# Delta-rule blocks: k-k and k-q products by halves with the heads alternating and fillers pinned between their turns, and three small moves of loads and copies

## The chip, the cores and the metric

The kernel runs on one core of a Trainium2 chip. The metric is the device time of one execution in microseconds (us). Before the change the median of three runs is 1339.09 us (1338.87 to 1339.35). The engines of the core run their own instruction streams in order: TensorE (PE) multiplies, VectorE (DVE), ScalarE (ACT) and GpSimd (POOL) do the rest, and SyncE (SP) and ScalarE issue the DMA transfers.

## The reference, cut to what matters

A block of a transformer with two mixers side by side: eight heads of dilated attention and eight heads of a gated delta rule, then a gated feed-forward part. The change lies in the delta rule and in the projections that run beside it.

```python
def reference(x, c, w_ada, ..., w_gate, w_up, w_down, final_norm_g):
    mod = c_act @ w_ada[l] + b_ada[l]
    h = _rmsnorm(x, norm_attn_g[l]) * (1.0 + sc1) + sh1
    proj = h @ w_in[l]
    q_a, k_a, v_a, q_d, k_d, v_d, z_d, b_d, a_d = jnp.split(proj, ...)
    y_attn = _dilated_attention(q_a, k_a, v_a, rel_bias)
    y_delta = _gated_deltanet(q_d, k_d, v_d, z_d, b_d, a_d, ...)
    x = x + g1 * (jnp.concatenate([y_attn, y_delta], axis=-1) @ w_out[l])
    h = _rmsnorm(x, norm_ffn_g[l]) * (1.0 + sc2) + sh2
    x = x + g2 * ((jax.nn.silu(h @ w_gate[l]) * (h @ w_up[l])) @ w_down[l])
    return _rmsnorm(x, final_norm_g)

def _gated_deltanet(q, k, v, z, ...):
    qkv = jax.nn.silu(_causal_conv(jnp.concatenate([q, k, v], axis=-1), conv_w))
    ...
    o = _chunk_gated_delta_rule(q, k, v, g, beta)
    return _rmsnorm(o, norm_g) * jax.nn.silu(z)

def _chunk_gated_delta_rule(q, k, v, g, beta):
    decay = jnp.where(causal, jnp.exp(gcum[..., :, None] - gcum[..., None, :]), 0.0)
    a_mat = jnp.where(strict, jnp.einsum('nbhcd,nbhed->nbhce', k_beta, kc) * decay, 0.0)
    sol = lax.linalg.triangular_solve(a_mat + eye, rhs, lower=True, ...)
    qk = jnp.where(causal, jnp.einsum('nbhcd,nbhed->nbhce', qc, kc) * decay, 0.0)
    ...
    _, o = lax.scan(step, state0, (qc, kc, u, w, gcum, qk))
```

There are 1024 tokens of 1024 features. A delta head has 64 features. The kernel works on chunks of 128 tokens where the reference has 64; the result is the same function.

## The kernel before, in words

**Groups.** The eight delta heads are worked on in two groups (g = 0 and 1) of four heads. A tile of k or q holds two heads, one on partitions 0 to 63 and the other on 64 to 127 (`kd[hp]`, `qd[hp]`), and eight chunks of 128 tokens along its rows. `delta(g)` runs: the convolutions and the transposes for the norms (`conv`, `delta_turn`), then `delta_prep`, `delta_v`, `delta_inverse` and `delta_scan`.

**The k-k and k-q products** (`delta_prep`, line 806). For each pair of heads q (two pairs in a group), for k-q ("q") and then k-k ("k"), for each half hf of the eight chunks, a turn of eight products of 64 x 128 by 64 x 128 is issued, four for each head e, into one PSUM bank for each head. Half 0 takes the two banks "s", half 1 the two banks "t". VectorE multiplies each full bank by the decay of that head (line 812). The decay is made in place in `lts` by 32 exponentials on ScalarE (line 776), head by head, eight chunks each. The finished k-k tiles go to DRAM (line 819) and come back as rows (`nt`, line 859). A program of 31 steps on VectorE (lines 905 and 909) inverts blocks of 32, its result goes to DRAM and comes back (`tn`, line 914), and four "heads" of small products (`lv`, `lw`, `lx`, lines 937 to 975) join the blocks on TensorE.

**Fillers.** Beside that run projections that don't depend on it: `others()` is a generator that issues matmuls of 512 or 256 columns (`gemm`, line 591, and `proj_t`, line 617) and yields after 0.64 or 0.32 us of them, in the order k and q of group 1, z of group 0, v of group 1, then v of the attention, z of group 1, k and q of the attention and so on. `turn(name)` first draws `FILL[name]` us out of this generator and then lets its instructions stand behind the last matmul drawn (`issue_after`). `hold(what, us)` at the start of the joining of the inverse draws until a projection is done and then `LEVELS` us more; the first product of the inverse stands behind that. `mixed()` also runs bursts of the modulation's matmuls after each 7.6 us of filler, unless `quiet` is set. What the delta part doesn't draw is drawn evenly by the attention (`attend`, constants `FRONT` and `BACK`).

**Order.** A scheduler takes the program's instructions by priority (the order of writing, `urgent()` puts them ahead) and puts each on its engine's stream when its operands are to be had in its own reckoning; the order on each engine is then fixed. Only `issue_after` pins an instruction behind another.

**The small places.** `z_evac` (line 638) copies a finished z block out of its PSUM bank through a Silu on ScalarE. `delta_early` starts the convolutions of group 1 (`cv0` to `cv3`) while group 0 inverts. `spill` (lines 1146 to 1151) copies projections of group 1 to DRAM. `out_delta` (lines 1475 to 1489) runs the delta half of the output projection during the attention: for each of eight row blocks d it splits a weight slab, and for each half it loads a block of x into `xo` (line 1482), multiplies, adds (line 1486) and stores. `xo`, `y_load`'s tiles and the first attention outputs share five buffers.

Of the kernel before, what the change touches and what calls it, by code (L numbers as in the profile page):

```python
# [10 lines left out]
F32 = mybir.dt.float32  # L11
# [20 lines left out]
LEVELS = ("z0", 4), ("z1", 24)  # L32
# [17 lines left out]
    "kk1_0_0_q": 6.4,  # L50
    "trq1_0False": 4.48,
    "trk1_0False": 1.92,
    "kk0_2_0_k": 1.28,
# [4 lines left out]
    "kk1_3_0_k": 0.64,  # L58
    "y0_0": 0.64,
    "trv3_0": 12.8,  # L60
    "kk1_0_0_k": 0.64,
# [5 lines left out]
    "kk0_0_0_k": 0.64,  # L67
}
for step in "abcd":
    for h in range(4):  # L70
        FILL.setdefault(f"l{step}0_{h}", 0.64)


def build(tc, I, out):
# [476 lines left out]
    def conv(ci, xp, dst):  # L551
        nc.scalar.activation(dst, xp, AF.Copy, scale=cw[:, ci, 3:4])
# [10 lines left out]
    used = [0.0]  # L563

# [18 lines left out]
    def gemm(ps, slabs, mh, ml, cs):  # L583
# [3 lines left out]
        for (wh, wl), k0 in slabs:  # L587
            for k4 in range(4):
                w0 = slice(k4 * P, (k4 + 1) * P)
                for a, b in ((wh, mh), (wh, ml), (wl, mh)):  # L590
                    last[0] = nc.tensor.matmul(ps, a[:, w0], b[k0 + k4][:, cs], start=(i == 0), stop=(i == n - 1))  # L591
                    i += 1
# [10 lines left out]
    def proj_t(src, n, name, evac, slabs=()):  # L603
# [5 lines left out]
        for tb in range(TB):  # L609
# [3 lines left out]
            for k in range(KT):  # L613
                wh, wl = slabs[k // 2]
                w0 = slice((k % 2) * n, (k % 2) * n + n)
                for a, b in ((hh, wh), (hl, wh), (hh, wl)):
                    last[0] = nc.tensor.matmul(ps[:, :n], a[k][:, ts_], b[:, w0], start=(i == 0), stop=(i == 23))  # L617
# [15 lines left out]

    def z_evac(g):
        def f(tb, ps):
            zt = pv.tile([P, 256], F32, name=f"zt{g}_{tb}", tag="ev", bufs=4)
            with urgent():
                taken[0] = nc.scalar.activation(zt, ps[:, 0:256], AF.Silu)  # L638
# [120 lines left out]
    def delta_prep(g, st, norms, kt, lts):  # L759
# [14 lines left out]
        for h in range(4):  # L774
            for n in range(8):
                nc.scalar.activation(lts[h][:, n], lts[h][:, n], AF.Exp, bias=lr[:, n, h : h + 1])
# [15 lines left out]
        qks = []  # L792
        for q in range(2):
# [3 lines left out]
            for dsts, mov, wh in ((two, qd[hp], "q"), (lts[2 * q : 2 * q + 2], kd[hp], "k")):  # L797
                for hf in range(2):

                    ps = [(sbank, tbank)[hf](f"kk{g}_{2 * q + e}_{hf}_{wh}") for e in range(2)]  # L800
                    with turn(f"kk{g}_{2 * q}_{hf}_{wh}"):
                        for j in range(4):
                            n = 4 * hf + j
                            for e in range(2):
                                rows = slice(64 * e, 64 * e + 64)
                                nc.tensor.matmul(
                                    ps[e][:, j * P : (j + 1) * P], kd[hp][rows, n * P : (n + 1) * P],
                                    mov[rows, n * P : (n + 1) * P], start=True, stop=True,
                                )
# [17 lines left out]

        for q in range(2):
# [310 lines left out]
    def spill(name, dst, scale=None):  # L1139
        def f(hf, ps):  # L1140
            for i in range(2):
# [8 lines left out]
                with held() if scale else urgent():  # L1150
                    (nc.sync if scale else nc.scalar).dma_start(
# [253 lines left out]
    def att_value(hp, n, ets):  # L1405
# [30 lines left out]
        if hp < EARLY:  # L1436
            t = pa.tile([P, HALF], F32, name=f"yo{hp}_{n}", tag="xo", bufs=5)
# [37 lines left out]
    def out_delta():  # L1475

        for d in range(KT):
# [614 lines left out]
```

## Time and profile before

| what | time |
|---|---|
| median of three runs | 1339.09 us |
| lowest and highest | 1338.87, 1339.35 us |
| the profiled execution | 1340.85 us |
| its span, first to last instruction | 1339.1 us |
| mean granted clock of TensorE | 0.996 |
| TensorE busy | 1309.2 us |
| VectorE busy | 837.6 us |
| ScalarE busy | 617.8 us |

The projections and the delta part fill the span up to about 450 us, the attention and the output projection up to about 697 us, and the feed-forward part the rest. In the rows of a timeline the columns are the start, the duration, the engine, the line, the operation, what is written from what, and the count; in brackets stands the idle time before and what ended it. In the rows of a table by windows they are the window, its length, and for each engine the busy time and the number of instructions, then the granted clock, the DMA share and the GB/s. A matmul of fp32 operands leaves two records. A matmul's duration in these rows reaches over the start of the next one, so a pace is read from starts.

### The profile page before, as it was taken

How to read it: one execution, taken by the hardware profiler on the slowest of the kernel's cores; microseconds unless marked ns; L12 is line 12 of the kernel's file. 1: busy time of each engine (PE TensorE's matmuls, PEld its weight loads, DVE VectorE, ACT ScalarE, POOL GpSimd, SP SyncE). 2: the span in 40 equal slices, each digit the busy share in tenths (PEclk: the TensorE clock that was granted, in tenths of full speed). 3: DMA queues.
4: the chain of work that ended last, by engine and by line, in shares of the span. 5: the costliest groups of instructions: out<-in, count | busy, mean ns of one | idle time of the engine just before them, and what ended most of it. 6: DMA issues, size and time to landing. Idle time of an engine off the chain costs nothing.

```text
span 1339.1 us, 25018 instructions
## 1 busy us (share of the span) xinstructions
PE 1309.2 (98%) x9440; PEld 1067.3 (80%) x9440; DVE 837.6 (63%) x1609; ACT 617.8 (46%) x1238; POOL 237.2 (18%) x241
## 2 busy tenths in 40 slices
PE   8999999999999999999999999999999999999997
PEld 5777787898988877667878788888888888888876
DVE  3685674666946221554379967576666675474597
ACT  4497513338232333543577433333333333444565
POOL 2344403333212423333610000000000000000000
PEclk9999998999999999999999999999999999999999
DMA  8625665467442455663654546354444665665685
GB/s 324 233 67 179 182 204 159 135 180 205 141 140 79 129 154 158 195 187 111 196 177 127 187 162 198 111 198 148 141 158 166 208 216 204 234 223 192 202 267 195
DMA packets 188520, 236.82 MB, mean 177 GB/s; under 512 B 48494, under 2 KB 96079, under 8 KB 188400
## 3 DMA queue, kind: packets, MB, share of 16 engines
q1 hardware_dynamic: 180336, 227.89, 53.3%
q10 hardware_dynamic: 8064, 7.34, 1.6%
q8 instruction: 74, 1.21, 0.4%
q14 instruction: 46, 0.38, 0.1%
HBM read 172.37 MB, written 62.92 MB: 176 GB/s over the span
## 4 chain that ended last, share of the span: by engine, by line
PE 79%; DVE 9%; DMA 6%; ACT 2%; issue 2%; POOL 1%; SPq 1%; ACTq 0%; DVEq 0%; POOLq 0%
PE wua L1681 9%; PE wga L1681 9%; PE X L1883 7%; PE wo L591 6%; PE wgc L1681 4%; PE wuc L1681 4%; PE Z L1883 4%; PE g_a L591 4%; PE f L247 3%; PE wgb L1681 2%; PE Y L1883 2%; PE wub L1681 2%; DVE tm L905 2%; PE g_va L617 2%; DVE tt L909 2%; PE vd L499 2%
## 5 line engine op out<-in xcount | busy, mean ns | idle before, releaser
L1671 DVE TENSOR_TENSOR wl_db<-wr_db,wh_db 128x512 fp32r<-128x512 f32 x77 | 52.9, 691 | 67.1 <-ACT wh_db L1670 66.8
L1670 ACT CAST wh_db<-wr_db 128x512 fp32r<-128x512 f32 x77 | 47.6, 622 | 88.9 <-PE X L1883 37.8
L1370 DVE CUSTOM_DVE_ANT_0 X<-S,bt 128x128 f32<-128x128 f32 (+7 forms) x64 | 30.8, 517 | 73.3 <-PE S L1365 48.6
L1883 PE MATMUL X<-wl_db,wh_da 128*128 128x512 f32 x160 | 62.4, 390 | 0.3 <-DVE wl_db L1671 0.3
L1883 PE MATMUL X<-wh_db,wh_da 128*128 128x512 f32 x160 | 62.3, 389 | 0.0
L1883 PE MATMUL X<-wh_db,wl_da 128*128 128x512 f32 x160 | 62.2, 389 | 0.0
L591 PE MATMUL wo<-yh,wh_wo 128*128 128x512 f32 x128 | 53.3, 417 | 2.1 <-DVE xo L1486 2.1
L1374 ACT ACTIVATE X<-X,sc 128x128 f32<-128x128 f32 (+7 forms) x64 | 37.0, 579 | 39.1 <-DVE sc L1370 39.1
L1671 DVE TENSOR_TENSOR wl_da<-wr_da,wh_da 128x512 fp32r<-128x512 f32 x77 | 52.9, 687 | 2.1 <-ACT wh_da L1670 2.1
L1376 POOL TENSOR_SCALAR X<-X,sc 128x128 f32<-128x128 f32 (+7 forms) x64 | 35.6, 563 | 95.8 <-DVE sc L1375 90.5
L1670 ACT CAST wh_da<-wr_da 128x512 fp32r<-128x512 f32 x77 | 47.5, 617 | 10.5 <-DMA wr_da<-ao_d 4.2
L591 PE MATMUL wo<-yl,wh_wo 128*128 128x512 f32 x128 | 50.9, 398 | 0.4 <-DVE yl L1501 0.3
L591 PE MATMUL g_a<-hh,wh_a 128*128 128x512 f32 x128 | 51.1, 400 | 0.0
L591 PE MATMUL wo<-yh,wl_wo 128*128 128x512 f32 x128 | 51.0, 398 | 0.0
L591 PE MATMUL g_a<-hl,wh_a 128*128 128x512 f32 x128 | 50.3, 393 | 0.0
L591 PE MATMUL g_a<-hh,wl_a 128*128 128x512 f32 x128 | 50.1, 391 | 0.0
L1670 ACT CAST wh_wg_s<-wg_s 128x512 fp32r<-128x512 f32 x33 | 20.6, 623 | 56.2 <-PE wuc L1681 23.8
L1670 ACT CAST wh_wu_s<-wu_s 128x512 fp32r<-128x512 f32 x33 | 20.4, 622 | 44.1 <-PE wga L1681 17.2
L1670 ACT CAST wh_wg<-wr_wg 128x512 fp32r<-128x512 f32 x31 | 19.2, 622 | 46.0 <-PE wua L1681 18.9
L617 PE MATMUL g_va<-wh_va,hh 128*128 128x256 f32 x128 | 38.2, 298 | 0.0
L617 PE MATMUL g_va<-wl_va,hh 128*128 128x256 f32 x128 | 38.1, 298 | 0.0
L617 PE MATMUL g_z<-wh_z,hh 128*128 128x256 f32 x128 | 36.7, 287 | 1.4 <-ACT zt L638 1.4
(552 smaller groups left out, 4143.1 us busy)
## 6 DMA issues: line engine op xcount, KB each, us to landing
wm<-in_wada SPq DMA_DIRECT2D x44, 512.0 KB, 5.3
wr_da<-ao_d SPq DMA_DIRECT2D x77, 256.0 KB, 2.8
wr_wu<-in_wu SPq DMA_DIRECT2D x50, 256.0 KB, 2.7
wr_wg<-in_wg SPq DMA_DIRECT2D x48, 256.0 KB, 3.1
ao_d<-a SPq DMA_DIRECT2D x44, 256.0 KB, 2.5
wr_wd<-in_wdn SPq DMA_DIRECT2D x44, 256.0 KB, 2.7
wr_db<-wt_d SPq DMA_DIRECT2D x44, 256.0 KB, 3.1
ao_d<-as SPq DMA_DIRECT2D x33, 256.0 KB, 2.0
```

The costliest lines, as they stand in the source:

```text
L247: nc.tensor.matmul(first[bank], a[:, w0], b[k][:, cs], start=(k == 0 and n_ == 0), stop=(k == KT - 1 and n_ == 2))
L499: nc.tensor.matmul(banks[j], a[:, w0], b[k][:, cs], start=(k == 0 and n_ == 0), stop=(k == KT - 1 and n_ == 2))
L591: last[0] = nc.tensor.matmul(ps, a[:, w0], b[k0 + k4][:, cs], start=(i == 0), stop=(i == n - 1))
L617: last[0] = nc.tensor.matmul(ps[:, :n], a[k][:, ts_], b[:, w0], start=(i == 0), stop=(i == 23))
L905: nc.vector.tensor_tensor(out=tv, in0=bc(nt[:, j, j + 1 : 32], j + 1), in1=tt[:, j, 0 : j + 1].unsqueeze(1).to_broadcast([P, m, j + 1]), o ...
L1370: nc.vector.tensor_tensor_reduce(out=x[:, 0:w], in0=pss[e][:, 0:w], in1=bt[:, e, 480 - w : 480], scale=1.0, scalar=3e38, op0=ALU.add, op1= ...
L1374: nc.scalar.activation(x[:, 0:w], x[:, 0:w], AF.Exp, scale=-1.0, bias=sc[:, 0:1], accum_out=sc[:, 2:3])
L1376: nc.gpsimd.tensor_scalar(out=x[:, 0:w], in0=x[:, 0:w], scalar1=sc[:, 3:4], scalar2=0.0, op0=ALU.mult, op1=ALU.add)
L1670: nc.scalar.copy(hi, src)
L1671: (eng or nc.vector).tensor_tensor(out=lo, in0=src, in1=hi.bitcast(F32), op=ALU.subtract)
L1681: nc.tensor.matmul(ps, a[:, w0], b, start=(first and k == 0 and n_ == 0), stop=(k == 3 and n_ == 2), skip_group_check=True,)
L1883: nc.tensor.matmul(bank[b], a[:, ts_], w, start=(first and n_ == 0), stop=(last and n_ == 2), skip_group_check=True,)
```

## The change

1. `delta_prep` runs the products by halves: for each pair of heads, for each half, k-q and then k-k. The k-q turns take the banks "s" and the k-k turns the banks "t". Within a turn each product stands behind the one before it (`issue_after`), so that heads strictly alternate. From the third turn of a group on, the first filler matmul that a turn draws stands behind the last product of the turn before (`pin`, `pinned()` in `gemm` and `proj_t`), and `quiet` is set over the turns.
2. The exponentials run in the same order: for two heads the first half of the chunks, then the second.
3. `FILL` and `LEVELS`: 8.96 us ahead of the first turn of group 0, 12.8 us ahead of the second turn of group 1, 0.64 us ahead of six turns of each group; the old entries of these turns go. The levels rise from 4 to 8 and from 24 to 28 us.
4. The first convolution of `delta_early` stands behind the z eviction of token block 6 of group 0.
5. The spill of v of group 1 is issued by SyncE, not by ScalarE.
6. `out_delta` asks for both halves of x ahead of the weight slab, with `urgent()`, and the shared buffers become six.

```diff
-LEVELS = ("z0", 4), ("z1", 24)
+LEVELS = ("z0", 8), ("z1", 28)
...
-    "kk1_0_0_q": 6.4,
+    "kk1_0_0_k": 12.8,
+    "kk0_0_0_q": 8.96,
...
-    "kk0_2_0_k": 1.28,
...
-    "kk1_3_0_k": 0.64,
...
-    "kk1_0_0_k": 0.64,
...
-    "kk0_0_0_k": 0.64,
 }
+for turn in ("0_1_q", "0_1_k", "2_0_q", "2_0_k", "2_1_q", "2_1_k"):
+    for g in range(2):
+        FILL[f"kk{g}_{turn}"] = 0.64
...
-    def conv(ci, xp, dst):
-        nc.scalar.activation(dst, xp, AF.Copy, scale=cw[:, ci, 3:4])
+    def conv(ci, xp, dst, behind=None):
+        with tc.issue_after(behind.ins) if behind else ExitStack():
+            nc.scalar.activation(dst, xp, AF.Copy, scale=cw[:, ci, 3:4])
...
+    pin = [None]
+
+    def pinned():
+        mm, pin[0] = pin[0], None
+        return tc.issue_after(mm.ins) if mm else ExitStack()
...
-                    last[0] = nc.tensor.matmul(ps, a[:, w0], b[k0 + k4][:, cs], start=(i == 0), stop=(i == n - 1))
+                    with pinned():
+                        last[0] = nc.tensor.matmul(ps, a[:, w0], b[k0 + k4][:, cs], start=(i == 0), stop=(i == n - 1))
...
-        for h in range(4):
-            for n in range(8):
-                nc.scalar.activation(lts[h][:, n], lts[h][:, n], AF.Exp, bias=lr[:, n, h : h + 1])
+        for h0 in (0, 2):
+            for hf in range(2):
+                for h in (h0, h0 + 1):
+                    for n in range(4 * hf, 4 * hf + 4):
+                        nc.scalar.activation(lts[h][:, n], lts[h][:, n], AF.Exp, bias=lr[:, n, h : h + 1])
...
+        mm, quiet[0] = None, True
         for q in range(2):
...
-            for dsts, mov, wh in ((two, qd[hp], "q"), (lts[2 * q : 2 * q + 2], kd[hp], "k")):
-                for hf in range(2):
-
-                    ps = [(sbank, tbank)[hf](f"kk{g}_{2 * q + e}_{hf}_{wh}") for e in range(2)]
+            for hf in range(2):
+                for dsts, mov, wh in ((two, qd[hp], "q"), (lts[2 * q : 2 * q + 2], kd[hp], "k")):
+                    ps = [(sbank if wh == "q" else tbank)(f"kk{g}_{2 * q + e}_{hf}_{wh}") for e in range(2)]
+                    pin[0], mm = mm if q + hf else None, None
                     with turn(f"kk{g}_{2 * q}_{hf}_{wh}"):
                         for j in range(4):
                             n = 4 * hf + j
                             for e in range(2):
                                 rows = slice(64 * e, 64 * e + 64)
-                                nc.tensor.matmul(
-                                    ps[e][:, j * P : (j + 1) * P], kd[hp][rows, n * P : (n + 1) * P],
-                                    mov[rows, n * P : (n + 1) * P], start=True, stop=True,
-                                )
+                                with tc.issue_after(mm.ins) if mm else ExitStack():
+                                    mm = nc.tensor.matmul(
+                                        ps[e][:, j * P : (j + 1) * P], kd[hp][rows, n * P : (n + 1) * P],
+                                        mov[rows, n * P : (n + 1) * P], start=True, stop=True,
+                                    )
...
+        pin[0], quiet[0] = None, False
...
-                    (nc.sync if scale else nc.scalar).dma_start(
+                    (nc.sync if scale or name[0] == "v" else nc.scalar).dma_start(
...
-            conv((4 if kind == "k" else 0) + 2 + q, fetch(j, f"{kind}{2 + q}"), t)
+            conv((4 if kind == "k" else 0) + 2 + q, fetch(j, f"{kind}{2 + q}"), t, zts[0, 6] if j == 0 else None)
...
+            xos = [pa.tile([P, HALF], F32, name=f"xo{d}_{hf}", tag="xo", bufs=6) for hf in range(2)]
+            for hf, xo in enumerate(xos):
+                with urgent():
+                    nc.sync.dma_start(xo, I["xT"][d * P : (d + 1) * P, hf * HALF : (hf + 1) * HALF])
             slabs = [(wsplit(I["wo"][d, 1], 512, f"wo{d}_1"), 4)]
-            for hf in range(2):
+            for hf, xo in enumerate(xos):
                 cs = slice(hf * HALF, (hf + 1) * HALF)
-                xo = pa.tile([P, HALF], F32, name=f"xo{d}_{hf}", tag="xo", bufs=5)
-                nc.sync.dma_start(xo, I["xT"][d * P : (d + 1) * P, cs])
```

More of the change, by code (lines that the diff above doesn't have):

```diff
@@ L616, in proj_t @@
                 for a, b in ((hh, wh), (hl, wh), (hh, wl)):
-                    last[0] = nc.tensor.matmul(ps[:, :n], a[k][:, ts_], b[:, w0], start=(i == 0), stop=(i == 23))
+                    with pinned():
+                        last[0] = nc.tensor.matmul(ps[:, :n], a[k][:, ts_], b[:, w0], start=(i == 0), stop=(i == 23))
                     i += 1
@@ L632, in build @@
             nc.scalar.copy(xps[2 + q][:, cs], ps)
+    zts = {}
     def z_evac(g):
```

6 lines of the change are left out of this document (3 added, 3 removed).

## The prediction, made before the result

> **What bounds the kernel now.** I read the page first, then the waits of TensorE, then the granted clock by stretches of 4 us, and last the timelines of single engines where TensorE stood still.
>
> ```profile
> PE 1309.2 (98%) x9440; PEld 1067.3 (80%) x9440; DVE 837.6 (63%) x1609; ACT 617.8 (46%) x1238; POOL 237.2 (18%) x241
> PEclk9999998999999999999999999999999999999999
> ```
>
> TensorE is busy 98% of the span, so the time is its work plus its standing still. An edit can gain only where it shortens the work itself, removes a wait of this engine, or keeps its clock up. The page also shows one slice below 9 in the clock. The waits of TensorE that the edits touch, and the clock around that slice:
>
> ```profile
> PE wo L591 <- DVE xo L1486: 2.1, 1, 2.1
> PE g_z L617 <- ACT zt L638: 1.4, 1, 1.4
> PE lw L967 <- ACT tc L959: 0.9, 1, 0.9
> PE lv L953 <- DVE cs L949: 0.8, 1, 0.8
> PE kk_q L806 <- DVE qk L812: 0.8, 1, 0.8
> PE kk_k L806 <- DVE qk L812: 0.4, 1, 0.4
> PE kk_q L806 <- DVE dt L812: 0.3, 1, 0.3
> 216.00:220.00 4.00, 4.00 (x54) 2.94 (x54) 1.51 (x3) 1.29 (x3) 2.17 (x2) 0.80 0.35 128
> 220.00:224.00 4.00, 4.00 (x36) 2.90 (x37) 1.77 (x5) 1.15 (x3) 0.30 (x1) 0.50 0.13 46
> 224.00:228.00 4.00, 4.00 (x65) 2.90 (x57) 0.00 (x0) 2.49 (x8) 1.27 (x1) 0.50 0.42 131
> 228.00:232.00 4.00, 4.00 (x60) 3.34 (x56) 2.41 (x5) 0.00 (x0) 0.95 (x1) 0.92 0.00 0
> ```
>
> The waits are 6.7 us in all. The clock column (0.80, 0.50, 0.50, 0.92) says that 4 x (0.20 + 0.50 + 0.50 + 0.08) = 5.1 us of TensorE's time are lost in these 16 us, although it is called busy.
>
> **The k-k and k-q products.** This is the largest edit. First what they take now, in group 0 and group 1, and how they run:
>
> ```profile
> 121.00:151.00 30.00, 11.91 (x128) 10.30 (x128) 1.00 0.64 193
> 312.00:328.00 16.00, 12.42 (x128) 11.06 (x128) 1.00 0.71 178
> 136.46 0.40 PE L591 MATMUL g_kd<-hh,wl_kd 128*128 128x512 f32 x1
> 136.79 1.16 PE L806 MATMUL kk_q<-qd,kd 64*128 64x128 f32 x8
> 137.87 0.50 PE L591 MATMUL g_qd<-hh,wh_qd 128*128 128x512 f32 x1
> 138.21 0.39 PE L591 MATMUL g_qd<-hl,wh_qd 128*128 128x512 f32 x1
> 138.44 0.39 PE L591 MATMUL g_qd<-hh,wl_qd 128*128 128x512 f32 x1
> ...
> 140.59 0.27 PE L806 MATMUL kk_k<-kd 64*128 64x128 f32 x1
> 140.59 0.27 PE L806 MATMUL kk_q<-qd,kd 64*128 64x128 f32 x1
> 140.70 0.27 PE L806 MATMUL kk_k<-kd 64*128 64x128 f32 x1
> 140.70 0.27 PE L806 MATMUL kk_q<-qd,kd 64*128 64x128 f32 x1
> ...
> 142.58 1.71 PE L806 MATMUL kk_k<-kd 64*128 64x128 f32 x16
> ```
>
> 128 records take 11.91 us in group 0 (93 ns each) and 12.42 us in group 1 (97 ns): 24.3 us together. Where two products of different halves of the partitions stand beside each other, two records start every 0.11 us: 55 ns each. A run such as the x16 at 142.58 takes 1.71 us, 107 ns each: the scheduler put the four products of one head one behind the other. The change forces head 0, head 1, head 0, head 1. Fully paired that is 256 x 55 ns = 14.1 us, a gain of 10.2 us; not paired at all it gains nothing. I take 60 ns, close to the paired rows with something left for the start of each turn: 15.4 us, **-9.0 us**.
>
> The price: a change of kind. From the last g_kd to the first kk is 0.33 us, from the first g_qd to the next 0.34 us, against 0.23 us in a row (138.21 to 138.44): 0.21 us for going there and back. Now there are 8 runs of such products with something else between (five and three, counted in TensorE's timeline); after it 7 and 8, because six turns in each group have a filler of 0.64 us in front. 7 more cost **+1.5 us** (ends 0 and 3).
>
> Each turn (16 records, 0.96 us, then three fillers, 0.68 us, and the change, 0.21 us) lasts about 1.85 us. It must cover the eviction of two heads and eight exponentials in every two turns:
>
> ```profile
> 139.00:152.00 13.00, 9.92 (x16) 1.00 0.43 115
> 139.69 8.28 ACT L776 ACTIVATE dt<-dt,lr 128x128 f32<-128x128 f32 x28
> 131.60 6.97 DVE L554 SCALAR_TENSOR_TENSOR vd<-xp_v,cw,vd 128x1023 f32<-128x1023 f32 x3
> ```
>
> 16 evictions of VectorE are busy for 9.92 us, 0.62 us each, so 1.24 us a turn. An exponential takes 8.28 / 28 = 0.30 us, 2.4 us for the eight of two turns (3.7 us). Both fit, and the new order (the first half of two heads before the second half) lets the first evictions start after 4 and 8 exponentials. So the three waits (1.5 us) should go. But the order on TensorE is now rigid: the fillers stand pinned between the turns, and nothing can pass. A convolution of v between two evictions (6.97 us for three instructions) is longer than the two turns of slack that the two pairs of banks give. I put 1.5 us of new waits in their place: **0** in sum, ends -1.5 and 12 (one us at each of the twelve pinned turns).
>
> **The filler and the inverse.** Fillers are projections that must be done anyway, so moving them costs nothing by itself. They decide what is late next. Ahead of the k-k turns stand 8.96 + 6 x 0.64 = 12.8 us in group 0, and 12.8 + 3.84 = 16.6 us in group 1 (before: 7.04). Behind the turns comes the inverse, a chain on VectorE and through DRAM, which ends with the landing of tn:
>
> ```profile
> 128.94 0.28 PE L787 MATMUL ps_bp<-ident,nbp 128*32 128x128 f32 x1 [0.79 <-DVE nbp L780]
> 150.53 0.65 PE L881 MATMUL trv<-ident,vd 128*128 128x128 f32 x4
> 205.67 1.79 DVE L942 STREAM_TRANSPOSE U<-tn 32x256 f32<-32x256 f32 x4 [0.95 <-DMA tn<-tn_d]
> 210.60 0.69 PE L937 MATMUL lv<-tn,dt 32*32 32x32 f32 x32
> 379.08 1.78 DVE L942 STREAM_TRANSPOSE U<-tn 32x256 f32<-32x256 f32 x4 [7.13 <-DMA tn<-tn_d]
> ```
>
> Group 0: the turns end at 150.53 now. After the change, from the transpose of bp at 128.94 (0.28 us): 60 fillers at 0.227 us (13.6 us), 128 records at 60 ns (7.7 us), 7 changes (1.5 us) and 1 us of transposes give 153.0, 2.5 us later. If the chain moves with it, tn lands at 208.2 in place of 205.67. The first product of the inverse (210.60) stands behind a fixed amount of filler, of which the level adds 4 us: seven yields, 21 matmuls, 4.8 us. It moves by -4.2 (pairing) + 0.4 (two changes) - 1.1 (two waits) - 1.4 (the z wait below) + 4.8, to 209.1. So slack shrinks from 4.9 us to about 0.9 us. The transposes take 1.79 us, the two cs behind them 0.9 us, and the second product of the inverse, due about 210.4, waits some **+0.9 us** (ends 0 and 3.4, if the turns end 2.5 us later still).
>
> Group 1: tn lands at 379.08 and TensorE is waiting there; this is the wait of 0.8 us (lv on cs). The level of 28, the 4 us of group 0 and 9.6 us more filler in the turns push the inverse's place back by up to 17.6 us of filler, while the chain moves by that 9.6 us less half the pairing. The wait goes: **-0.8 us**. The same 17.6 us are missing in the attention's front, where they are spread over 14 units, 1.3 us less each. No wait of TensorE stands there now, so I cost it at nothing; the cover is the rest of the filler, and 0.5 us at each unit would be 7 us.
>
> **The small parts.**
>
> ```profile
> 198.71 1.15 ACT L552 ACTIVATE cv<-xp_k,cw 128x1024 f32<-128x1024 f32 x1 [6.49 <-DMA tn_d<-tt]
> 200.18 0.39 PE L617 MATMUL g_z<-wh_z,hh 128*128 128x256 f32 x1 [1.42 <-ACT zt L638]
> 213.53 1.65 ACTq L1151 DMA_DIRECT2D pj_d<-sp_vd  x2
> 215.56 0.36 ACT L959 COPY tc<-lv 32x256 f32<-32x256 f32 x1 [1.78 <-issue]
> 582.82 5.00 DMA xo<-in_xT
> 587.84 0.76 DVE xo L1486
> ```
>
> ScalarE waited 6.49 us with cv at its head, and the eviction of z stood behind it. Pinned behind the z eviction of block 6, cv can't do that: **-1.4 us**. cv itself comes 1 to 2 us later; behind it stand three VectorE operations, which ended before tn landed.
>
> The copy at 215.56 sat 1.78 us behind two issues of the vd spill on ScalarE's queue, and TensorE waited 0.9 us for it. With the spill on SyncE the copy can run at 215.56 - 1.78 = 213.8: **-0.9 us**. The eight issues go to SyncE, where they hold up weight loads by at most 0.4 us each; nothing there was due.
>
> The load of xo left at 582.82 and landed 5.00 us later; TensorE waited 2.1 us. Both halves are now asked for ahead of the slab, with a sixth buffer: **-2.1 us** (ends -2.1 and +2.6). The upper end: SyncE is in order, and an urgent load that waits for a free buffer holds the weight slabs behind it for as long as one wait of that kind there.
>
> ```profile
> SPq L225 <- POOL wl_wo L227: 4.9, 2, 2.6
> ```
>
> **The clock.** A mean of 0.80 over four us is half the clock from 218.4 on, 2.4 us after the wait of 0.9 us, among products of 32 and 64 rows. My term for it is 0: the wait goes, but the new one before the second product, just as long, stands in the same place. Ends -5.1 (it goes) and +5.1 (a second one, in the turns). The Trainium skill, "TensorE: Matmul & The Clock Gate", Part 1, has the clock halve only after about 3.4 us of idle. By that rule the 0.9 us is not the cause, and removing it returns nothing (1327.3); by the place of the dip it returns 5.1 us (1322.2). No wait near the dip is longer than 1.4 us and the clock fell nevertheless, so this trace doesn't bear the rule out as worded; it bears out the halves.
>
> **The sum.** -9.0 + 1.5 + 0 + 0.9 - 0.8 - 1.4 - 0.9 - 2.1 = -11.8 us. The profiled execution took 1340.85 us, its span 1339.1 and 1.75 around it, 1.76 above the median of 1339.09. From the median: **1327.3 us**.
>
> **The rivals.**
> - The clock stays up as well (the dip hung on the wait, as its place suggests): 5.1 us more, 1322.2. Against it: the new wait in that place. Chance 0.27.
> - The products don't pair, though they alternate: each turn is held by the bank of one head, so records still come at 95 ns. Then the 9.0 us fall away: 1336.3. For it: the mean of 93 to 97 ns now, although the program's loop names the heads in turn already. Against it: the pairs at 140.59 and 140.70. Chance 0.15.
> - Slower: ScalarE and VectorE set the pace of the turns. If table loads and the convolutions of v come between exponentials and evictions, TensorE stands at every pinned turn. It decides from 12 us of such waits, one us a turn; with the three convolution instructions of 6.97 us falling twice into each group, less 2 x 1.85 us of slack, it is 4 x 3.3 = 13 us, and a second dip of 5.1 us: 1345. For it: the rigid order. Against it: 16 evictions now fit in 13 us. Chance 0.12.
> - Others (the attention's front starved by some us, one small part without effect): 1328 to 1340, 0.06.
>
> The forecast of 1327.3 has 0.40. A measurement of this kernel tells about 0.2% (2.7 us) from no change. Faster than that: 0.40 + 0.27 + half of the pairing rival + most of the others, 0.79. Within it 0.09, slower 0.12. The range takes in the clock rival with 4 us more, and reaches just past the pairing rival: 1318 to 1338.
>
> **What would show it.** The windows of L806: 128 records in 7 to 8 us of each group, if paired; 12 us if not. The waits of TensorE for qk and dt: under 2 us in all, else VectorE sets the pace. No wait of g_z for zt, of lw for tc, of wo for xo. lv or lw in group 0 waiting about 1 us, if the chain is as late as I think; more than 4 us would break the forecast. The granted clock between 210 and 235 separates the first two cases. tr, y or S waiting for ET or X between 440 and 540 would show a starved front.

## The result, and the profile after

| | before | after |
|---|---|---|
| median of the runs | 1339.09 us (5 runs, 1337.66 to 1358.71) | 1358.05 us (4 runs, 1352.82 to 1364.11) |
| ratio, 95% interval | | 1.0135 [1.0106, 1.0164] |
| the profiled execution, its span | 1340.85, 1339.1 us | 1360.41, 1358.7 us |
| TensorE standing still (waits) up to the first wga | 20.4 us | 33.2 us |
| clock lost up to the first wga | 5.1 us | 10.2 us |

Executions more than 1.5% above the fastest of their kernel are left out of the ratios; here that is the run of 1358.71 us of the kernel before and a fifth run of the change (4505.69 us, unexplained, in no median either), and in the table further down the profiled runs of e5 and e8, two more of e8, which therefore has no ratio, one of e10 and five of e14.

The change makes the kernel 1.35% slower by the ratio (19 us between the medians); 1327.3 had been forecast, with a range to 1338. From the first `wga` of the feed-forward part on both take the same time within 0.6 us, so the loss lies ahead of it: in the profiled execution the first `wga` starts 19.0 us later (716.54 against 697.58), with 12.8 us more of standing still and 5.1 us more of lost clock. "Clock lost" is the sum of (1 - granted clock) over windows of 0.5 us; for whole runs, below, it is span x (1 - mean clock), which in the 16 profiles holds 0.6 to 3.9 us more, lost behind the first `wga`.

The page after, engines and clock:

```profile
PE 1315.8 (97%) x9440; PEld 1067.3 (79%) x9440; DVE 842.7 (62%) x1609; ACT 617.7 (45%) x1238; POOL 241.3 (18%) x241
PEclk9999999998999999999999999999999999999999
```

The dent of before (seventh digit) is gone and another stands three slices later, about 310 to 320 us, at the turns of group 1. Of the waits of TensorE after, those ahead of the first `wga` that are new or longer than before (line, for what; us in total, times, the longest; a choice):

```profile
PE yt L1100 <- DVE o L1090: 4.5, 7, 2.4
PE trq_0False L754 <- ACT cv L559: 4.4, 2, 3.4
PE g_a L599 <- ACT sp_a L1165: 3.4, 2, 1.8
PE tr L1412 <- POOL X L1392: 2.1, 2, 1.2
PE trk_0True L754 <- ACT sqq L760: 1.9, 1, 1.9
PE kk_q L821 <- ACT sqq L760: 1.8, 1, 1.8
PE y L1442 <- ACT et L1416: 1.7, 1, 1.7
PE trv L897 <- ACT vd L559: 1.6, 1, 1.6
PE g_va L626 <- ACT va L1144: 1.3, 1, 1.3
PE lv L969 <- DVE cs L965: 1.0, 1, 1.0
```

The waits that the small parts were to remove (g_z on zt, lw on tc, wo on xo) are gone, and so are those on qk and dt in the turns. In their place stand longer ones, most of them on ScalarE. The longest, read from the timelines of TensorE (last filler, then the transposes of q) and ScalarE:

```profile
305.10 0.28 PE L626 MATMUL g_va<-wl_va,hh 128*128 128x256 f32 x1
308.83 0.55 PE L754 MATMUL trq_0False<-ident,cv 128*128 128x128 f32 x3 [3.45 <-ACT cv L559]
...
305.74 0.60 ACT L760 ACTIVATE sqq<-trq_1False 128x512 f32<-128x512 f32 x1
306.43 1.28 ACT L559 ACT_TABLE_LOAD   x1
307.72 1.06 ACT L559 ACTIVATE cv<-cv 128x1024 f32<-128x1024 f32 x1
```

ScalarE has squares, a table load and the Silu of cv to do, and TensorE, which asks for cv, has no filler left that it may draw: the next stands behind a turn that waits for cv. What follows is read from a table by windows of 3.41 us (window, length, busy time of PE, PEld, DVE, ACT, POOL, then the granted clock):

```profile
302.62:306.03 3.41, 2.76 (x24) 2.56 (x22) 1.72 (x4) 3.02 (x8) 1.42 (x2) 1.00 1.02 372
306.03:309.44 3.41, 0.61 (x6) 0.61 (x7) 1.03 (x2) 3.29 (x4) 1.53 (x1) 1.00 0.87 285
309.44:312.86 3.42, 1.91 (x8) 0.99 (x6) 0.80 (x5) 1.22 (x3) 0.00 (x0) 0.50 1.02 352
316.27:319.68 3.41, 3.41 (x18) 2.52 (x16) 0.00 (x0) 1.51 (x4) 1.91 (x1) 0.50 0.76 210
319.68:323.10 3.42, 3.38 (x30) 2.69 (x32) 1.49 (x3) 3.42 (x12) 1.91 (x1) 1.00 0.88 213
```

TensorE is busy for 0.61 us of one window; the next three run at half clock, and 5.1 us are lost beside the wait of 3.45. The clock's steps are explained below.

### The profile page after: what moved, and what is told of

Same layout as the page of the kernel before. It is cut to its first block, busy times and chain, and to the rows that moved or that the text cites. A ratio compares the mean times of both kernels' runs of the same rounds, so it can differ in the third digit from the quotient of the medians.

```text
span 1358.7 us, 25036 instructions
## 1 busy us (share of the span) xinstructions
PE 1315.8 (97%) x9440; PEld 1067.3 (79%) x9440; DVE 842.7 (62%) x1609; ACT 617.7 (45%) x1238; POOL 241.3 (18%) x241
## 4 chain that ended last, share of the span: by engine, by line
PE 76%; DVE 11%; DMA 7%; issue 2%; ACT 2%; POOL 1%; SPq 1%; ACTq 0%; DVEq 0%; POOLq 0%
PE wua L1699 9%; PE wga L1699 8%; PE wo L599 6%; PE X L1901 6%; PE g_a L599 5%; PE wuc L1699 4%; PE wgc L1699 4%; PE Z L1901 3%; PE f L247 2%; PE wgb L1699 2%; PE Y L1901 2%; PE wub L1699 2%; DVE tt L925 2%; DVE tm L921 2%; PE y L1442 2%
## 5 line engine op out<-in xcount | busy, mean ns | idle before, releaser
L1688 ACT CAST wh_wg_s<-wg_s 128x512 fp32r<-128x512 f32 x33 | 20.5, 623 | 55.8 <-PE wuc L1699 23.8
L1688 ACT CAST wh_wu_s<-wu_s 128x512 fp32r<-128x512 f32 x33 | 20.4, 622 | 44.6 <-PE wga L1699 17.2
L227 POOL TENSOR_TENSOR wl_wo<-wr_wo,wh_wo 128x512 fp32r<-128x512 f32 x24 | 31.1, 1297 | 50.1 <-ACT wh_wo L226 42.3
L1688 ACT CAST wh_wu<-wr_wu 128x512 fp32r<-128x512 f32 x33 | 20.5, 622 | 37.9 <-issue 24.1
```

The lines of the kernel that those rows point to most:

```text
L227: (eng or nc.gpsimd).tensor_tensor(out=lo[:, :n], in0=raw[:, :n], in1=hi[:, :n].bitcast(F32), op=ALU.subtract)
L1688: nc.scalar.copy(hi, src)
```

## The experiments

Medians, the ratio to runs of the kernel before on the same chip, and means over the runs. "Rest" is the time less the clock loss.

| run | what it is | median us (range) | ratio [95%] | clock loss | rest |
|---|---|---|---|---|---|
| before | | 1339 to 1342 | | 3.8 to 4.4 | 1336.3 to 1337.5 |
| after | the change | 1358.05 (1352.82 to 1364.11) | 1.0135 [1.0106, 1.0164] | 11.9 | 1346.4 |
| e4_again | the change again | 1357.22 (1352.87 to 1360.44) | 1.0129 [1.0099, 1.0159] | 10.5 | 1346.4 |
| e1_small | before + small parts | 1338.12 (1331.74 to 1343.97) | 0.9980 [0.9959, 1.0000] | 4.4 | 1333.8 |
| e7_spill | before + spill on SyncE | 1340.36 (1335.65 to 1342.10) | 0.9993 [0.9973, 1.0013] | 3.9 | 1335.8 |
| e2_core | after - small parts | 1355.74 (1350.40 to 1359.18) | 1.0111 [1.0073, 1.0149] | 7.8 | 1347.5 |
| e3_oldfill | after, old filler and levels | 1346.05 (1344.24 to 1357.59) | 1.0064 [1.0029, 1.0098] | 14.4 | 1334.5 |
| e5_nopin | after - pins | 1359.35 (1349.96 to 1371.21) | 1.0118 [1.0066, 1.0171] | 15.7 | 1344.3 |
| e6_pair | before + alternation | 1359.62 (1355.41 to 1371.98) | 1.0154 [1.0086, 1.0221] | 22.8 | 1338.8 |
| e8_halves | after, old filler, no pins | 1357.67 (1334.99 to 1359.90) | none | 24.8 | 1327.8 |
| e11_noalt | e8 - alternation | 1356.32 (1342.33 to 1360.48) | 1.0092 [1.0055, 1.0129] | 20.5 | 1333.7 |
| e9_fill | before, new filler and levels | 1351.28 (1344.28 to 1354.59) | 1.0061 [1.0038, 1.0084] | 8.5 | 1341.7 |
| e10_level | before, new levels | 1356.85 (1347.52 to 1376.50) | 1.0109 [1.0068, 1.0151] | 14.4 | 1344.9 |
| e13_turnfill | after, old levels | 1373.59 (1367.88 to 1386.81) | 1.0251 [1.0200, 1.0303] | 24.4 | 1351.0 |
| e12_g0 | e1 + alternation in group 0 | 1337.28 (1333.33 to 1339.57) | 0.9966 [0.9949, 0.9982] | 2.9 | 1334.1 |
| e14_low | e12, level of group 1 at 20 | 1359.03 (1339.85 to 1380.12) | 1.0090 [1.0055, 1.0125] | 32.5 | 1329.8 |

Medians, losses and rests of the experiments are over all runs of the range given. The rest isn't a time that the kernel would reach: at half clock TensorE's waits shrink, so a run with a large loss has too small a rest.

### First: which part of the change costs

**e1_small** is the kernel before with parts 4, 5 and 6 of the list above; **e2_core** is the change without them; **e4_again** is the change once more.

```diff
+        conv(..., t, zts[0, 6] if j == 0 else None)
...
-                    (nc.sync if scale else nc.scalar).dma_start(
+                    (nc.sync if scale or name[0] == "v" else nc.scalar).dma_start(
...
+            xos = [pa.tile([P, HALF], F32, name=f"xo{d}_{hf}", tag="xo", bufs=6) for hf in range(2)]
...
```

> The kernel before with the three small parts alone: the convolution pinned behind the z eviction, the v spill issued by SyncE, both halves of x loaded early with six buffers. Theory A (the turns of the k-k and k-q products with their fillers cost the time): the small parts keep their 1.4 + 0.9 + 2.1 us, so 1333 to 1336 us, with the clock dip near 218 us gone perhaps 1329. Theory B (the late convolution or the loaded SyncE queue starts the new waits of the queries' transposes for cv): 1345 us or more, with waits of trq for cv over 3 us.

> The changed kernel without the three small parts: the turns by halves, the exponentials' order, the fillers and the levels stay. Theory A: 1360 us or a little more (1356 to 1368), since all of the loss is here and 4 us of gain are taken away. Theory B: 1335 to 1345 us.

> The changed kernel once more, on the same chip as the other three, since its runs lay 11 us apart (1352.8 to 1364.1) where those of before lie within 2. If this spread belongs to the program (waits of DMA and clock dips that fall differently from run to run), the runs lie between 1350 and 1365 again and the profile shows other places of waiting than the first. If it belonged to the chip or the hour, they agree within 2 us. Either way 1350 to 1362 us by both theories.

The small parts bring 0.2%, some 60% of what was forecast (-4.4), with an interval that reaches from 0 to 0.4%, and the change without them is as slow as with them. The loss is in the core, and it repeats: e4 has the same waits in the same places (trq on cv 3.4 at the longest, yt 2.4).

**e3_oldfill** keeps order, pins and small parts and takes the filler program of before.

```diff
-LEVELS = ("z0", 8), ("z1", 28)
+LEVELS = ("z0", 4), ("z1", 24)
-    "kk1_0_0_k": 12.8,
-    "kk0_0_0_q": 8.96,
+    "kk1_0_0_q": 6.4,
...
```

> The changed kernel with the filler table and the levels of before (6.4 us ahead of the first k-q turn of group 1, nothing between the other turns of group 0 but 1.28 us; levels 4 and 24); order by halves, pins and small parts stay. If the amount of filler drawn early causes the loss (chains late, a thin front of the attention): 1330 to 1342 us, and the waits of tr, y and g_a after 450 us go. If the rigid order of the turns causes it: 1350 us or more, with the waits of the transposes and k-q products for sqq still there.

11 to 12 us come back. The rest falls from 1346.4 to 1334.5, near that of the small parts alone (1333.8): as far as the rest can be read, order and pins cost little at full clock, and gain nothing. What is left against e1 is clock (14.4 for 4.4 us). In its profile TensorE waits 2.8 us for qd and 3.4 us for sqq at the first turns of group 0, and from 135 us on 13.7 us run at half clock.

### Second: the pins, the alternation, the halves, the dip

**e5_nopin**, the change without the pins:

```diff
-                    pin[0], mm = mm if q + hf else None, None
+                    mm = None
```

> The changed kernel, but no other product is pinned behind a turn any more: the halves, their order, the strict alternation of heads, the shorter filler programs and the small parts stay. Theory A (the pins are a barrier: once one filler product has to stand behind a turn, none that follows it in the one ordered stream can fill the waits of 1.8 to 3.5 us ahead of the turns, and the clock falls after each of these): the waits on cv, sqq and qd ahead of the turns go, with the dips behind them, at least 8 us in all; 1338 to 1348 us. Theory B (the loss is in how much filler is drawn early, so that attention and the scan of group 1 lack it): no more than 3 us come back, 1352 us or more, and the waits of the joining of group 1 and of attention stay as long as they are.

Nearer to the second theory: 1359.35 by the median, and 1.0118 for 1.0135. These are its waits in the turns:

```profile
PE kk_q L821 <- ACT sqq L760: 2.1, 2, 1.5
PE kk_q L821 <- DMA qd<-cv_d: 2.0, 1, 2.0
PE kk_k L821 <- DVE dt L827: 1.3, 1, 1.3
PE trq_0False L754 <- ACT cv L559: 1.0, 1, 1.0
```

The waits on cv fall from 4.4 to 1.0 us in all (before: 1.0), and with them goes the half clock at 310, so the wait of 3.4 us was made by the pins. But the one on sqq stays (2.1), new ones on the DMA of qd (2.0) and on dt (1.3) come, with 6.8 us of half clock from 341 on, and the yt wait of 2.4 us in the scan of group 1 is unchanged. The rest falls by 2 us only, not by 8: the barrier is real, and taking it away gains nothing to be seen in the time.

**e6_pair** is the kernel before with strict alternation inside each turn:

```diff
+                        mm = None
...
-                                nc.tensor.matmul(
...
+                                with tc.issue_after(mm.ins) if mm else ExitStack():
+                                    mm = nc.tensor.matmul(
...
```

> The kernel before, with one thing: inside each turn the k-k (or k-q) products of the two heads alternate strictly. No pins, no halves, no other filler. The forecast's term for this was 9.0 us (60 ns a record for 93 and 97): 1331 us if it stands, with no wait added. At the 68 ns a record that the changed kernel shows it is 24.3 - 17.4 = 6.9 us at most: 1333 to 1335. If what binds is not the order of the heads but the work beside them, it is 0: 1340.

20 us slower, which none of the three cases had. Two things are to be seen. The products do get faster, but little. This is the table by windows for their line alone in e8, both groups at full clock (after the length stand TensorE's busy time and its weight loads):

```profile
120.00:162.00 42.00, 10.21 (x128) 8.50 (x128) 1.00 0.65 190
300.00:340.00 40.00, 11.10 (x128) 8.91 (x128) 1.00 0.71 212
```

11.91 us became 10.21, 12.42 became 11.10: 3.0 us for both groups. An alternating run of 16 takes 1.09 us from its start to that of the filler behind it, 68 ns a record, as TensorE's timeline of the changed kernel shows:

```profile
149.69 1.16 PE L821 MATMUL kk_k<-kd 64*128 64x128 f32 x16
150.78 0.50 PE L599 MATMUL g_qd<-hh,wh_qd 128*128 128x512 f32 x1
```

And there is a new wait in the turns of group 1 (TensorE's timeline of e6, then VectorE's):

```profile
334.41 1.50 PE L808 MATMUL kk_k<-kd 64*128 64x128 f32 x15
338.84 2.45 PE L808 MATMUL kk_k<-kd 64*128 64x128 f32 x15 [2.93 <-DVE qk L814]
...
333.41 1.29 DVE L814 TENSOR_TENSOR qk<-kk_q,dt 128x512 f32<-128x512 f32 x2
335.29 2.90 DVE L554 SCALAR_TENSOR_TENSOR vd<-xp_v,cw,vd 128x1023 f32<-128x1023 f32 x1 [0.59 <-ACT vd L552]
338.11 1.27 DVE L814 TENSOR_TENSOR qk<-kk_q,dt 128x512 f32<-128x512 f32 x2
```

VectorE's queue has a convolution of v between two evictions. It waits 0.59 us for ScalarE and takes 2.90 us, and the next turn stands 2.93 us for its bank; before, the longest wait for a bank was 0.8 us, with the same convolution among the evictions. This wait of 2.93, 1.8 us for tn and 1.5 us on cs each stand ahead of a stretch of half clock; of the 23 us that its profile is longer, 18.8 are clock (23.9 for 5.1).

**e8_halves** is the change with the old filler and without pins, so the order by halves, the alternation and the small parts; **e11_noalt** takes the alternation out of it. The first two lines below are in both, the last two in e11 alone; both also have the filler lines of e3.

```diff
-                    pin[0], mm = mm if q + hf else None, None
+                    mm = None
...
-                                with tc.issue_after(mm.ins) if mm else ExitStack():
+                                with ExitStack():
```

> The changed kernel with the filler programs and levels of the kernel before and without the pins; the halves with their order, the exponentials in that order, the alternation and the small parts stay. It stands beside the run that had the old filler with the pins (1346). If the pins are the barrier: 8 us or more less than that run, 1330 to 1338 us, with no wait over 1.5 us on sqq or qd ahead of the turns. If the order by halves itself makes TensorE wait (ScalarE's squares and exponentials come later than the turns ask for them): within 3 us of it, 1343 to 1349 us.

> The run by halves with the old filler and no pins (1334.99 to 1359.90), without the strict alternation of heads; the halves with their order, the exponentials in that order and the small parts stay. If the alternation is what holds the banks of both heads until the end of a turn, so that VectorE and with it the chain to tn start later: the waits on tn, qk and S shrink, the clock stays up (0.997 on the mean), 1328 to 1335 us. If the order by halves does it: no different, 1335 to 1358 us, with the same waits and dips.

e8 met neither of its ranges: three runs lie at 1357 to 1360 us, one at 1334.99. The alternation isn't what sets the dip: both have it, at the same place. The products of e8 are 3.0 us shorter, but the inverse hangs on the last eviction of the turns, on VectorE. From the transpose of bp of group 1 to the end of that eviction it is 17.6 us before (312.96 to 330.55), 20.9 in e8 and 19.8 in e11, and the first reader of tn begins 48.5 to 51.2 us behind it in all three. Counted from that transpose, TensorE gets to the inverse 2.8 us later in e8 and 3.4 in e11, and the first reader of tn begins 4.5 and 4.9 us later. (Of TensorE's delay 1.0 us is a burst of the modulation, 32 matmuls, that stood elsewhere before: `quiet` is set in both and was never run alone. Another 1.6 us in e8 is a wait for vd, 1.1 us in e11 one for sp_a.) The difference is a wait; the waits of e11 have it so:

```profile
PE lv L953 <- DMA tn<-tn_d: 1.5, 1, 1.5
```

From there, 379 to 427 us, e11 runs at half clock (e8: 378.5 to 433). The fastest run of e8, 1334.99, has nearly no clock loss (0.999); it lies 3.1 us under the median of the small parts alone and over their fastest (1331.74). One run doesn't settle whether the order by halves would gain without the dip.

**e7_spill** has the spill of v on SyncE and nothing else.

> The kernel before, with the spills of v issued by SyncE in place of ScalarE and nothing else. This wait was 0.9 us and a stretch of half clock began behind it. If the dip hangs on that wait: 6 us less (0.9 of waiting and 5.1 of clock), 1334 to 1335 us, and the clock of the stretch from 216 to 230 us stays whole. If the dip comes of something else there: 0.9 us less, 1339 to 1340 us, and the dip stays.

0.9993: no change, and the mean clock loss (3.9) is that of before (4.1 on the same chip). The wait of lw for tc is gone in its profile, and nothing is gained by it. The dip at 218 us, on which a rival of 0.27 rested, was a matter of the one execution that had been profiled: its mean clock was 0.996, and 22 of the 28 other runs of the kernel before on these two chips (1 and 4) have 0.997 or more, too high for a loss of 5.1 us.

### Third: the filler

**e9_fill** gives the kernel before the new `FILL` and `LEVELS`; **e10_level** the two levels alone; **e13_turnfill** takes the levels back out of the change.

> The kernel before with the new filler programs and levels alone; the products, their order and everything else as before. Theory F (the loss is in the filler: some 18 to 26 us of it are drawn ahead of the attention that then lacks it): with the clock losses of the records taken off, 8 to 12 us more than before; 1345 to 1352 us, at least 5 us of it between the first S and the first wga. Theory O (filler is work that must be done anyway, and the loss comes of the new order of the products): within 3 us of before, 1337 to 1343.

> The kernel before with the levels of 8 and 28 in place of 4 and 24 and nothing else: 8 us more filler in the joining of the two groups, 8 us less in attention. If what attention lacks costs by its amount, this third of the filler that the whole change draws early costs a third of it, 2.5 to 4 us: 1341 to 1344. If attention stands only past a point, 0 to 1 us: 1339 to 1340.

> The changed kernel with the levels of before (4 and 24) and nothing else; the filler pinned ahead of the turns, the halves and the pins stay. If the levels are what starves attention: the stretch from the first S to the first wga comes out 4 to 6 us shorter than in the changed kernel, 1346 to 1353 us. If the filler in the turns does it: no shorter by more than 2 us, 1354 to 1360 us.

Filler that is drawn early costs by itself: by the ratio e9 is 0.61% (8 us) slower than before, and its rest is 4.2 us above before, that of e10 7.4. The time of e9 is what was expected of a loss in the filler (1345 to 1352), but its parts are smaller than expected: 4.2 us of rest for 8 to 12, and 3.3 us between the first S and the first `wga` for 5 or more. Without any pin, e9 also has the wait of the turns on sqq, and 10.2 us at half clock begin at 143 us, beside it:

```profile
PE kk_q L806 <- ACT sqq L749: 2.0, 2, 1.5
```

e10 and e13 went against what was expected of them. A third of the filler (6.1 us at S) cost more than all of it (16.6), though the intervals of e10 and e9 touch, and without the levels the change is 15 us slower, not faster; 12 us of that are clock, and its lv waits 3.4 us for tn. I read this so: 16.6 us of filler in the turns of group 1 delay the chain, the levels cover what this makes late, and attention then pays. No run shows the first two steps apart. What attention pays stands in this table, from TensorE's timelines: filler drawn before the first S, against before (matmuls by 0.227 us for 512 columns and 0.119 for 256), and the time from the first S to the first wga, less its filler and its clock loss, against before:

| program | filler drawn by S | S to wga |
|---|---|---|
| e14 | -3.7 us | -5.6 us |
| before, e7, e6 | 0 | 0, -1.9, -1.3 |
| e3, e11, e12, e1, e8 | 0 to 0.1 | -2.8, -3.1, -3.3, -3.9, -3.9 |
| e10 | +6.1 | +4.7 |
| e13 | +8.2 | +2.2 |
| after, e4, e2, e5, e9 | +16.3 to 16.9 | +3.3, +2.7, +3.0, +2.8, +3.3 |

The third row has the new xo loads, which the second has not: about 2 us. All programs with more filler ahead of S stand above all without: the change by 6 to 7 us above the third row, e9 by 3.3 us above the kernel before, neither of which has the new loads. In the changed kernel the waits of TensorE between S and `wga` are 6.5 us, in e1 2.2. The new ones are g_a on sp_a (1.8), tr on X (1.2 and 0.8) and y on et (1.7), at 504 to 621 us. Waits of tr, y or S for ET or X are what the prediction had named as the sign of a starved front, though it looked for them by 540 us. The other 3 us aren't waits, and I can't place them.

The longest wait of the second half lies ahead of the first S (480.89), in the scan of group 1, where the filler is used up too: yt (TensorE's timeline, then VectorE's and GpSimd's):

```profile
469.29 0.39 PE L599 MATMUL g_a<-hh,wl_a 128*128 128x512 f32 x1
472.08 0.41 PE L1100 MATMUL yt<-ident,o 128*128 128x128 f32 x2 [2.41 <-DVE o L1090]
...
466.19 0.43 DVE L1090 TENSOR_TENSOR o<-o,zl 128x256 f32<-128x256 f32 x1
...
468.83 0.16 DVE L1085 SCALAR_TENSOR_TENSOR of<-of,eq 128x4 f32<-128x4 f32 x1
470.11 0.43 DVE L1089 TENSOR_TENSOR o<-o,of 128x256 f32<-128x256 f32 x1 [1.12 <-ACT wh_a L226]
470.57 1.37 DVE L1090 TENSOR_TENSOR o<-o,zl 128x256 f32<-128x256 f32 x1
...
469.07 1.01 POOL L1088 TENSOR_TENSOR of<-of,mhalf 128x4 f32<-128x4 f32 x1 [0.73 <-DVE of L1085]
470.18 1.47 POOL L227 TENSOR_TENSOR wl_a<-wr_a,wh_a 128x512 fp32r<-128x512 f32 x1
```

The chain of one scan chunk (VectorE, GpSimd, VectorE twice) takes 3.1 us from 468.83 on; its last piece took 1.37 us beside a split on GpSimd, and 0.43 in the chunk before. The filler in front of yt ends at 469.6; the longest wait of this kind before the change was 1.0 us.

### Fourth: what is left of the idea

**e12_g0** is e1 with the alternation in group 0 only; **e14_low** is e12 with 20 for 24 in the level of group 1.

```diff
+                                with tc.issue_after(mm.ins) if mm and g == 0 else ExitStack():
...
-LEVELS = ("z0", 4), ("z1", 24)
+LEVELS = ("z0", 4), ("z1", 20)
```

> The kernel before with the three small parts, and strict alternation of heads in group 0 alone. With alternation alone the stretch of the turns of group 0 came out 2.2 us shorter and that of group 1 3.5 us longer, clock aside. If the gain of group 0 stands without group 1: 2 us less than the three small parts alone (1338.1), 1335 to 1337. If the earlier end of the turns only moves the wait to the inverse of group 0 (1.5 us on cs, and a dip behind it): 1340 to 1350.

> The kernel with the three small parts and alternation in group 0 alone (1337.3), with the level of group 1 lowered from 24 to 20. If filler left for attention pays steadily, as the levels of 8 and 28 cost steadily: 2 us less, 1334 to 1336, unless the inverse of group 1, now 4 us sooner, waits for tn. If it waits there by more than 2 us, a stretch of half clock follows in the inverse: 1345 to 1360.

e12 is 0.34% faster than the kernel before, and so the fastest of all that ran; against e1 (0.9980) the intervals overlap, so whether the alternation adds to the small parts isn't settled. Its profile has no stretch of half clock up to 700 us.

e14 shows the edge on which the old level stands. In e12 TensorE reaches the inverse of group 1 at 374.67 and tn's first reader begins at 374.72; in the kernel before it was 379.03 and 379.08. Four us less filler, and it waits. The wait of e14, and then its table by windows:

```profile
PE lv L942 <- DMA tn<-tn_d: 4.1, 1, 4.1
```

```profile
372.57:375.98 3.41, 0.74 (x46) 0.74 (x48) 0.65 (x2) 0.75 (x2) 0.08 (x1) 1.00 1.18 228
...
375.98:423.76 47.78, 47.78 (x603) 40.09 (x595) 14.81 (x37) 10.68 (x28) 3.77 (x5) 0.50 0.28 85
423.76:427.17 3.41, 3.41 (x30) 3.41 (x31) 2.24 (x9) 0.87 (x4) 1.01 (x1) 1.00 0.00 0
```

A wait of 4.1 us, and then 47.78 us of the inverse at half clock, 23.9 us lost, with TensorE busy all the time. Most of the matmuls in it are products of 32 and 64 rows, with fillers, bursts of the modulation and at the end the first products of the scan between them; in this stretch they didn't bring the clock back.

## Why the prediction was wrong

By the ratios the loss has two parts of about one size: the filler by itself costs 0.61% (e9), and order, alternation, pins and small parts with the old filler 0.64% (e3), the latter nearly all as clock. The profiled execution against that of before, by stretches: time less filler and less the modulation's matmuls (0.032 us each), from TensorE's timelines; the clock's part is in it.

| stretch | forecast | measured |
|---|---|---|
| start to the transpose of bp, group 0 | 0 | +1.2 |
| turns of group 0 and 1 | -7.5 | +7.9 (clock 6.2 of it) |
| between them: joining and scan of group 0 | -1.4 | -2.0 (the dip of before, 5.1, gone) |
| group 1, end of turns to the inverse | -0.8 | +4.1 |
| inverse and scan of group 1 | 0 | +2.7 (clock 1.7 of it) |
| attention, to the first wga | -2.1 | +5.1 (clock 1.7 of it) |
| sum | -11.8 | +19.0 |

**"I take 60 ns ... -9.0 us": the mechanism was right, the size wrong.** The products got 3.0 us shorter in e8. The 55 ns came from rows where a k-k and a k-q product stood beside each other; a run with the heads strictly alternating goes at 68 ns. And 93 to 97 ns were busy time divided by records, with the ends of short runs in it, which stay.

**"0 in sum" for the pinned turns: this step failed, and with it the place where waits were looked for.** I had asked whether VectorE's evictions and the exponentials fit into a turn. They do: no wait on qk or dt is left. But ScalarE's squares and table loads come *ahead* of and between the first turns. The waits there are 1.8 us on sqq in group 0, and in group 1 3.4 on cv and 1.9 on sqq (the last in neither e2 nor e4). That a pin takes away the filler which used to cover such a wait is shown for cv alone, by e5. The wait on sqq in group 0 stands without pins too (e5, and e9 with the old order), so it comes with the filler drawn ahead; e3 has a longer one with pins and the old filler. With the clock (6.2) these waits come near the 13 us that my slower rival priced; that is luck, since its mechanism, exponentials and evictions too slow for a turn, isn't what happened.

**"Fillers ... must be done anyway, so moving them costs nothing by itself", and the thin front "at nothing": failed.** This is the step with the clearest evidence. Taking the old filler back returns 11 to 12 us (e3); e9 and e10 cost 4 and 7 us of rest without any other edit. In attention my own sentence had the price, 0.5 us at each of 14 units, 7 us; the table above says 6 to 7 against the programs with the small parts, 3.3 for e9. That the figure comes so near is partly luck: the waits found make up 4 us of it.

**Group 1, "the wait goes: -0.8": the wait did go**, and others came in the stretch ahead: TensorE stood 1.7 us for sp_a at 369 and 1.3 us for va at 394, fillers whose evictions ScalarE had not done yet.

**Clock, "0, ends ±5.1": the dips lay elsewhere.** Over the runs the loss rose from about 4 to about 11 us. The Trainium skill, "TensorE: Matmul & The Clock Gate", Part 1, has a free-running window of 3413 ns by which the clock is set, and has it halve after about one idle window. The grid agrees with these runs (next but one section); "idle" does not. My end of 5.1 us was the one dip that I saw, and e14 shows 23.9 us behind one wait.

**What came as forecast:** the waits of g_z, lw, xo and of lv in group 1 went; the new wait of lv on cs in group 0 was 1.0 us (0.9 forecast; the forecast's own figures, 208.2 + 1.79 + 0.9 against 210.4, give 0.5, and no row has the 210.4). As time the three small parts give about 2.7 us of 4.4, with an interval from 0 to 5.5.

**Open:** four kernels besides the change (e2, e6, e9, e13) reach the first vd, 68 us in, 2.2 to 3.2 us later than before, though in e6 the edit lies wholly behind that point; they wait 1.4 to 1.6 us in all for the split of wl_f on GpSimd, the kernel before 0.2. I didn't find why. Open too is why a third of the filler (e10) costs more than all of it; in e10's profile 2.4 us are a wait of TensorE for va ahead of the inverse of group 1, and 4.7 fall in attention.

## What to carry to other kernels

A wait on TensorE has a price that depends on what comes next: ahead of dense filler often 1.7 us of clock, ahead of a long run of small products up to 14 times that; so leave slack ahead of such runs first. Filler is a budget: every piece drawn early to cover one chain is missing for another, and a pin or a fixed order takes it away even where it is left. Before paying for a faster turn, ask which engine ends it; here the chain behind the turns hung on VectorE's last eviction, and TensorE's 3.0 us brought nothing to be seen.

## What the hardware showed that I had not expected

In 14 of the 16 profiles the clock falls somewhere between 70 and 690 us, 37 times in all. Within one execution every fall and rise lies on one grid of 3.413 us (in the changed kernel all eight edges leave 2.25 to 2.29 when divided by it), and the grid's phase differs between executions. TensorE's busy time in a window of that grid goes with the clock of the next window, clearly at both ends and not in between:

| PE busy in a window at full clock | windows | next one at half clock |
|---|---|---|
| under 1.58 us of 3.41 | 20 | 20 |
| 1.58 to 2.55 | 99 | 17 |
| over 2.55 | 2296 | 0 |

So no wait need be 3.4 us long: the wait of 0.9 us of the kernel before lay in a window with 2.53 us busy. Nor does busy time alone settle it: in e11 the window of the 1.5 us wait for tn had 1.97 us busy and 47.8 us at half clock followed, in e3 the same wait (1.45 us) lay in a window with 1.96 us busy and the clock stayed. A wait of 1.8 us may fall into one window or be shared by two, which goes by the phase; that would explain runs of one program 18 us apart (e11: 1342.33 and 1360.48), but a run without a profile doesn't show its grid. Windows of small products seldom lift the clock, though TensorE counts as busy in all of them: e14 has 14 in a row at half clock.
